# Hybrid decoder block: the turns of k and q taken two to a step, k's second high half written by ScalarE, two gate groups moved forward

## Chip, cores and metric

The kernel runs on one core of one Trainium2 chip. The metric is the device time of one execution in microseconds (us), the median of several runs; lower is better. A profile of one execution stands beside the times.

## The reference

One decoder layer on x of shape 1 x 1024 x 1024, all in float32:

```
h = RMSNorm(x);  [q | k | v | u | g] = h @ W_in
A: 8 heads, q and k split into two halves of 64, QK-norm per half,
   p = softmax(q1 k1' * scale + bias) - lam * softmax(q2 k2' * scale + bias), causal
   a = RMSNorm(p @ v) * (1 - lam_init);  y_a = a @ W_pa
B: c = silu(LayerNorm(conv31(u_a * sigmoid(u_b))));  y_b = c @ W_pc
x = x + (sigmoid(g_a) * y_a + sigmoid(g_b) * y_b) @ W_out
x = x + SwiGLU(RMSNorm(x))
```

## The kernel before

**Products in parts.** Every float32 operand is split into a high part (rounded to the type that TensorE multiplies, written by ScalarE, `split_hi`, L120) and a low part (the rest, by VectorE, `split_lo`, L125). A product is three matmuls, high x high, high x low, low x high (`mm3`, L160 to L162). Score products pack more: a tile of k holds 64 rows of high parts and 64 rows of low parts, so that two matmuls (L1017, L1018) make one score product of a half head.

**Stages.** From 0 to about 315 us the normalised x is turned and most of the input projection runs (`opening`, then the list `first`). From 315 to about 823 us the attention runs in 64 steps, 8 heads by 8 blocks of 128 queries, in the order 4 5 6 7 0 1 2 3 within a head (`ORDER`; the last head 6 7 4 5 2 3 0 1). Then come the projection of a, LayerNorm and the projection of c, W_out, and the feed-forward in seven-product form.

**A step** n of the attention (the loop after L1176) issues: the score products of its block (`scores`; VectorE adds the bias tile `tb` and takes the minimum at L1019, ScalarE the exponential at L1024, VectorE joins the halves at L1033); a *group* of filling work, a piece of the input projection that is still to be made (`more`); the transposes of the block before (`turn`, tile pT, then the split into ph and pl); and the `slot`: products with v (`weigh`, tile pW), transposes back (`back`, pB), the subln (`subln_T`, pS, whose result goes to a_d in HBM), and the *late* work.

**Groups.** The list `later` says which projections fill which head's steps. An item Q has 4 groups (48 matmuls of 256 columns each): the q and k columns of the next head, in two blocks b=1 and b=0 of 512 tokens. An item G has 2 groups: one column tile of the gates for each half of the tokens, 24 matmuls of 512 columns each. A head has 8 steps; `groups(n)` gives one group to a step, and none to two of the steps where the head's list has only 6. Groups left over after step 63 run in `group()` twice and then in a loop over the rest, between the end of the scores and the projection of a.

**Late work: the turn.** After the second and fourth group of an item Q, two entries join the list `late`: the turn of k and the turn of q of that block (`turn_qk`). The order is k b=1, q b=1, k b=0, q b=0. Each entry has a first step: k b=1 may go at once, q b=1 and k b=0 from the middle of the head before (step 4 of its 8), q b=0 from the first step of its own head. A slot takes one entry (`min(nq, 1)`). A turn is: 4 transposes of 128 columns into a PSUM tile pQ (L770); ScalarE writes the high part s1 (L777); VectorE writes the low part (L779); then copies by DMA, all issued on SyncE's queue, bring halves of 64 partitions to where the score products want them. For q there are six: s2's two halves and s1's lower half from s1 (L780, L786, L787), the same for the low parts (L785, L786, L787). For k there are three: the lower half of s2 from s1 (L780), the upper half of s2 from the low part (L790), and the lower half of s1 from the low part (L791). The last overwrites what the first reads, so it waits for it. A wait of SyncE holds up all that stands behind it in its queue.

The next head's bias tile `tb` (L996, one buffer) is loaded by SyncE after the last L1019 of the head. The rest of SyncE's queue near a head's start are the weights of later groups (`wraw`), v (L987), and what the groups write to HBM.

**After the scores.** `early(h)` (L1207) loads a of heads 0 to 5 back from a_d into tiles that had held scores, splits them (aTh, aTl), and heads 6 and 7 follow (L1240) when pS of head 7 has been written. The projection of a takes heads 0 to 7 in this order into four banks (`o3`).

**Order.** A scheduler orders each engine's instructions when the program is built, by its own estimates of time; each engine then runs its list strictly in that order. `issue_after` binds some of it.

Of the kernel before, what the change touches and what calls it, by code (L numbers as in the profile page):

```python
# [12 lines left out]
AF = mybir.ActivationFunctionType  # L13
# [7 lines left out]
HD = 64  # L21
# [10 lines left out]
NT = S // P  # L32
# [25 lines left out]
def kernel(  # L58
# [28 lines left out]
    dve, act, pool, pe = nc.vector, nc.scalar, nc.gpsimd, nc.tensor  # L87
# [24 lines left out]
    def nm(s):  # L112
        uid[0] += 1
        return f"{s}_{uid[0]}"

    def f32(ap):
        return ap.bitcast(F32)
# [9 lines left out]
    def after(ins):  # L127

        return nullcontext() if ins is None else tc.issue_after(ins)
# [16 lines left out]
    def pg():  # L146
        npg[0] += 1
        p_, tag = pgs[npg[0] % len(pgs)]
        return p_.tile([P, 512], F32, tag=tag, name=nm("pg"))
# [4 lines left out]
    def pm(z="pm"):  # L154
        npm[0] += 1
        p_, tag = pms[npm[0] % len(pms)]
        return p_.tile([P, 512], F32, tag=tag, name=nm(z))
# [82 lines left out]
    def pcol(key, k=0):  # L240
        c = col[key] + k
        return pvec[:, c : c + 1]
# [114 lines left out]
    def gemm_N(o, halves, shi, slo, i):  # L357

        ts = slice(i * P, (i + 1) * P)
        for k in range(NKT):  # L360
            whi, wlo = halves[k // 4]
            mm3(o, kt(shi, k)[:, ts], kt(slo, k)[:, ts], whi[:, k % 4, :], wlo[:, k % 4, :], k == 0, k == NKT - 1)
# [18 lines left out]
    first = ["U1", "V1", "U2", "U3", "V2", "U4", "Q0", "V3", "U5", "U6", "U7"]  # L381
    later = [
        ["Q1", "G0", "G1"],
        ["Q2", "G2"],
        ["Q3", "G3"],
        ["Q4", "G4", "G5"],
        ["Q5", "G6"],
        ["Q6", "G7"],
        ["Q7", "G8", "G9"],
        ["G10", "G11", "G12", "G13"],  # L390
        ["G14", "G15"],
    ]
    TAPS_FIRST = 3.25

# [245 lines left out]
    def rstd_of(ss, n, scale, fast=False):  # L640
        v = sm.tile([P, 16], F32, tag="v", name=nm("v"))[:, :n]
        dve.tensor_scalar(v, ss, scale, EPS, op0=ALU.mult, op1=ALU.add)
        return rsq(v, n, fast)
# [97 lines left out]
    def q_item(h):  # L741
        halves = [ws.next(), ws.next()]
        t = {}
        T[h] = t
        for b in (1, 0):
            raw = qkp.tile([P, 4, 256], F32, tag="qkraw", name=nm("qkraw"), bufs=2)
            ss = sm.tile([P, 16], F32, tag="ss16", name=nm("ss16"))
            for i2 in range(2):
                o = pg()
                for e in range(2):  # L750
                    gemm_N(o[:, 256 * e : 256 * (e + 1)], halves, hT_hi, hT_lo, 4 * b + 2 * i2 + e)
                act.copy(raw[:, 2 * i2 : 2 * i2 + 2, :], o[:].rearrange("p (e c) -> p e c", c=256))
                jk = sm.tile([P, VD], F32, tag="jk", name=nm("jk"), bufs=1)[:, :HD]
                for g in range(8):
                    act.activation(
                        jk, o[:, g * HD : (g + 1) * HD], AF.Square, accum_out=ss[:, 8 * i2 + g : 8 * i2 + g + 1]
                    )
                if i2 == 0:
                    yield
            r = rstd_of(ss[:], 16, 1.0 / HD, fast=h > 0)  # L760
            r4 = raw[:].rearrange("p i (g d) -> p (i g) d", d=HD)
            dve.tensor_tensor(r4, r4, r.unsqueeze(2).to_broadcast([P, 16, HD]), op=ALU.mult)

            def turn_qk(z, key, b, raw):


                dma = nc.sync.dma_start
                pt = pm("pQ")
                for i in range(4):
                    pe.transpose(pt[:, i * P : (i + 1) * P], raw[:, i, z * P : (z + 1) * P], ident[:])  # L770
                w = pcol(key + "n")

                def part(j):
                    return qkp.tile([P, 512], F32R, tag=f"{key}s{j}", name=f"{key}s{j}_{h}_{b}", bufs=2 if key == "q" else 3)

                s1, s2 = part(1), part(2)
                act.activation(s1[:], pt[:], AF.Identity, scale=w)  # L777
                lo = part(3) if key == "q" else qkp.tile([P, 512], F32R, tag="klo", name=f"klo_{h}_{b}", bufs=1)
                dve.scalar_tensor_tensor(lo[:], pt[:], w, f32(s1[:]), op0=ALU.mult, op1=ALU.subtract)  # L779
                dma(f32(s2[HD:, :]), f32(s1[HD:, :]))  # L780
                if key == "q":
                    lo2 = part(4)
                    for one, two in ((s1, s2), (lo, lo2)):
                        if one is lo:
                            dma(f32(two[HD:, :]), f32(one[HD:, :]))  # L785
                        dma(f32(two[:HD, :]), f32(one[HD:, :]))  # L786
                        dma(f32(one[HD:, :]), f32(one[:HD, :]))  # L787
                    t["q", b] = (s1, lo), (s2, lo2)
                else:
                    dma(f32(s2[:HD, :]), f32(lo[HD:, :]))  # L790
                    dma(f32(s1[HD:, :]), f32(lo[:HD, :]))  # L791
                    t["k", b] = s1, s2

            for z, key in ((1, "k"), (0, "q")):
                free = NT * (h - 1) + (0 if key == "k" and b else NT if key == "q" and not b else NT // 2)
                late.append((free if h else 0, lambda a_=(z, key, b, raw): turn_qk(*a_)))
            yield
# [156 lines left out]
    n = 0  # L956
# [130 lines left out]
    def subln(h):  # L1087
        an = AN[h]
        r = rstd_of(SSA[h][:], NT, 1.0 / VD, fast=True)
        dve.tensor_tensor(an[:], an[:], r.unsqueeze(2).to_broadcast([P, NT, VD]), op=ALU.mult)  # L1090
# [18 lines left out]
    steps = [(h, i) for h in range(H) for i in ORDER[h]]  # L1109
    scm, weighs, backs, sublns = [], [], [], []  # L1110
    fill = run(it for l_ in later for it in l_)
    plan = [sum(4 if it[0] == "Q" else 2 for it in l_) for l_ in later]
# [15 lines left out]
    def ready(queue, n):  # L1128
        now = [e for e in queue if e[0] <= n]
        queue[:] = [e for e in queue if e[0] > n]  # L1130
        return [e[1] for e in now]

    def slot(n, nq):

        with after(last_fill[0]):
            for h, b, ar in ready(backs, n):
                back(h, b, ar)
                if b == ORDER[h][-1] // 2:
                    subln(h)
                    sublns.append((n + 1, h))  # L1140
            for _ in range(min(nq, 1)):
                if late[0][0] <= n:
                    late.pop(0)[1]()
            for h in ready(sublns, n):
                subln_T(h)
            for h, b in ready(weighs, n):
                backs.append((n + 2, (h, b, weigh(h, b))))
                if b == ORDER[h][-1] // 2 and h + 1 < H:
                    load_v(h + 1)

    def groups(n):

        return 0 if plan[n // NT] == 6 and n % NT in (5, 7) else 1

    def slack_of(n):

# [11 lines left out]
    for n, (h, i) in enumerate(steps):  # L1168
# [3 lines left out]
        nq = len(late)  # L1172
# [14 lines left out]
    n = len(steps)  # L1187
# [162 lines left out]
    for c in range(NE, NKT):  # L1350
        w = ws.next()
# [400 lines left out]
```

## Time and profile before

| what | value |
|---|---|
| runs | 1771.92, 1770.11, 1770.12 us; median 1770.12 us |
| the profiled execution | 1771.98 us, its span of instructions 1770.1 us |
| TensorE matmul (PE) busy | 1751.4 us of the span, 99% |
| VectorE (DVE) busy | 1274.1 us, 72% |
| ScalarE (ACT) busy | 798.9 us, 45% |
| DMA | 274.81 MB, mean 155 GB/s |
| mean granted clock of TensorE | 0.996 |

How to read it: a matmul's busy time overlaps that of the next, so that its pace is the distance from start to start, not its duration. "PEld" is the weight load. An idle time is put down to what ended it. Times in the timeline are from the start of the span.

### The profile page before, as it was taken

To read this page: it belongs to the slowest core of one execution; us is meant where nothing else is said; L and a number is where in the kernel's file an instruction comes from. 1 tells how busy PE (TensorE), PEld (TensorE's weight loads), DVE (VectorE), ACT (ScalarE), POOL (GpSimd) and SP (SyncE) were. 2 spreads that over 40 slices of the span, in tenths; PEclk is the share of its full clock that TensorE was granted. 3 is DMA by queue.
4 is the path that set the end of the run, shared out by engine and by line. 5 is a ranking of instruction groups with operands and counts; after the bars stand their busy time and mean duration, and the time that the engine had idled before them with its cause. 6 is when DMAs were issued, how large, how long until landed. Compare 5 with 4: busy or idle time off the path is not lost.

```text
span 1770.1 us, 25847 instructions
## 1 busy us (share of the span) xinstructions
PE 1751.4 (99%) x9377; PEld 1508.0 (85%) x9377; DVE 1274.1 (72%) x2167; ACT 798.9 (45%) x1879; POOL 28.9 (2%) x107
## 2 busy tenths in 40 slices
PE   9999999999999999999999999999999999999999
PEld 7898998999898998988887888888888888888887
DVE  7388879999888988887587534877667666665544
ACT  5111331657766767655456413643333333333332
POOL 2001000000000000000000000000000000000000
PEclk9999999999999999999999999999999999999999
DMA  6236362244444344454783544234544544697663
GB/s 206 96 118 215 103 190 97 79 122 112 111 117 134 102 111 120 111 138 150 250 291 102 167 164 150 92 101 143 173 155 150 174 155 146 200 358 250 215 214 131
DMA packets 254867, 274.81 MB, mean 155 GB/s; under 512 B 15970, under 2 KB 177802, under 8 KB 254740
## 3 DMA queue, kind: packets, MB, share of 16 engines
q1 hardware_dynamic: 252560, 266.40, 47.5%
q0 software_dynamic: 1744, 5.19, 1.1%
q8 instruction: 74, 1.21, 0.3%
q10 hardware_dynamic: 436, 1.58, 0.2%
q14 instruction: 53, 0.43, 0.1%
HBM read 176.07 MB, written 78.68 MB: 144 GB/s over the span
## 4 chain that ended last, share of the span: by engine, by line
PE 92%; DMA 4%; DVE 2%; ACT 2%; issue 1%; SPq 0%; ACTq 0%
PE acc L1606 22%; PE pg L160 14%; PE pg L161 14%; PE pg L162 14%; PE acc L487 12%; PE sc L1017 2%; PE sc L1018 2%; PE wo L160 2%; PE wo L162 2%; PE wo L161 2%; PE pT L1056 2%; DMA ks<-ks 1%; DMA gt<-g_d 1%; PE pW L160 1%; PE pW L161 1%; PE pW L162 1%
## 5 line engine op out<-in xcount | busy, mean ns | idle before, releaser
L561 DVE SCALAR_TENSOR_TENSOR acc<-u,cw,acc 128x1024 f32<-128x1024 f32 x240 | 306.6, 1278 | 2.9
L120 ACT CAST whi<-wraw 128x1024 fp32r<-128x1024 f32 x107 | 112.4, 1052 | 204.7 <-PE pg L161 116.4
L160 PE MATMUL pg<-hT_hi,whi 128*128 128x512 f32 x512 | 201.9, 394 | 0.0
L162 PE MATMUL pg<-hT_hi,wlo 128*128 128x512 f32 x512 | 201.2, 393 | 0.0
L161 PE MATMUL pg<-hT_lo,whi 128*128 128x512 f32 x512 | 200.9, 392 | 0.0
L161 PE MATMUL pg<-wlo,hT_hi 128*128 128x256 f32 x704 | 200.7, 285 | 0.0
L160 PE MATMUL pg<-whi,hT_hi 128*128 128x256 f32 x704 | 200.7, 285 | 0.0
L162 PE MATMUL pg<-whi,hT_lo 128*128 128x256 f32 x704 | 200.4, 285 | 0.0
L125 DVE TENSOR_TENSOR wlo<-wraw,whi 128x1024 fp32r<-128x1024 f32 x107 | 130.2, 1218 | 68.5 <-ACT whi L120 68.4
L125 DVE TENSOR_TENSOR wlo<-draw,whi 128x1024 fp32r<-128x1024 f32 x75 | 91.8, 1224 | 89.4 <-ACT whi L120 87.1
L120 ACT CAST whi<-draw 128x1024 fp32r<-128x1024 f32 x75 | 79.1, 1055 | 129.6 <-PE acc L487 121.0
L161 PEld LDWEIGHTS pg<-wlo,hT_hi 128*128 128x128 f32 x704 | 134.9, 192 | 2.0
L160 PEld LDWEIGHTS pg<-whi,hT_hi 128*128 128x128 f32 x704 | 134.9, 192 | 1.8
L162 PEld LDWEIGHTS pg<-whi,hT_lo 128*128 128x128 f32 x704 | 134.8, 192 | 1.4
L487 PE MATMUL acc<-wlo,whi 128*128 128x512 f32 x308 | 119.8, 389 | 0.0
L487 PE MATMUL acc<-whi,wlo 128*128 128x512 f32 x308 | 119.8, 389 | 0.0
L1024 ACT ACTIVATE E<-E,mn 128x640 f32<-128x640 f32 (+7 forms) x128 | 99.4, 778 | 38.2 <-DVE mn L1019 37.4
L162 PEld LDWEIGHTS pg<-hT_hi,wlo 128*128 128x128 f32 x512 | 96.2, 188 | 19.1
L161 PEld LDWEIGHTS pg<-hT_lo,whi 128*128 128x128 f32 x512 | 96.3, 188 | 18.7 <-issue 0.6
L160 PEld LDWEIGHTS pg<-hT_hi,whi 128*128 128x128 f32 x512 | 96.3, 188 | 18.7 <-issue 0.6
L1606 PE MATMUL acc<-h_lo,whi 128*128 128x512 f32 x240 | 93.4, 389 | 0.0
L1606 PE MATMUL acc<-h_hi,whi 128*128 128x512 f32 x240 | 93.4, 389 | 0.0
(292 smaller groups left out, 4031.6 us busy)
## 6 DMA issues: line engine op xcount, KB each, us to landing
wraw<-in_w_gate_up_dram SPq DMA_DIRECT2D x44, 512.0 KB, 4.6
wraw<-in_w_in_dram SPq DMA_DIRECT2D x40, 512.0 KB, 4.1
qs<-qs SPq DMA_DIRECT2D x96, 128.0 KB, 2.3
wd<-in_w_down_dram SPq DMA_DIRECT2D x44, 256.0 KB, 3.2
tdT<-wd SPq DMA_DIRECT2D x88, 128.0 KB, 4.5
draw<-sdS SPq DMA_DIRECT2D x44, 256.0 KB, 3.8
draw<-tdT SPq DMA_DIRECT2D x44, 256.0 KB, 3.8
wraw<-in_w_in_dram SPq DMA_DIRECT2D x32, 256.0 KB, 3.6
```

What stands on the lines that cost most here:

```text
L120: act.copy(dst, src)
L125: last_lo[0] = dve.tensor_tensor(dst, src, f32(hi), op=ALU.subtract).ins
L160: pe.matmul(o, lh, rh, start=start, stop=False)
L161: pe.matmul(o, lh, rl, start=False, stop=False)
L162: last_mm[0] = pe.matmul(o, ll, rh, start=False, stop=stop).ins
L487: m = pe.matmul(o[s_][i][:], l_[:, ts], r_[:, 512:], start=start and j + y_ == 0, stop=j == n - 1 and y_ == 2, skip_group_check=not start,)
L561: dve.scalar_tensor_tensor(acc[0][:], us[c][:, t : t + S], cw[:, c, t : t + 1], acc[0][:], op0=ALU.mult, op1=ALU.add)
L1017: pe.matmul(o[:, :w], qh[:, qs], k, start=True, stop=False)
L1018: last_mm[0] = pe.matmul(o[:, :w], ql[:, qs], k, start=False, stop=True).ins
L1024: act.activation(e[:, :nk], e[:, :nk], AF.Exp, bias=mn[:, j : j + 1], scale=-1.0, accum_out=l[:, j : j + 1])
L1056: pe.transpose(pt[:, k * P : (k + 1) * P], e[:, (k0 + k) * P : (k0 + k + 1) * P], ident[:])
L1606: pe.matmul(o[:], a_[x_][:, k, :], b_[y_][:, k, :], start=start and k + x_ + y_ == 0, stop=k == 3 and x_ == 1, skip_group_check=not start,)
```

## The change

```diff
     later = [
         ["Q1", "G0", "G1"],
-        ["Q2", "G2"],
-        ["Q3", "G3"],
-        ["Q4", "G4", "G5"],
-        ["Q5", "G6"],
-        ["Q6", "G7"],
-        ["Q7", "G8", "G9"],
-        ["G10", "G11", "G12", "G13"],
-        ["G14", "G15"],
+        ["Q2", "G2", "G3"],
+        ["Q3", "G4"],
+        ["Q4", "G5", "G6"],
+        ["Q5", "G7"],
+        ["Q6", "G8", "G9"],
+        ["Q7", "G10"],
+        ["G11", "G12", "G13", "G14"],
+        ["G15"],
     ]
...
                 lo = part(3) if key == "q" else qkp.tile([P, 512], F32R, tag="klo", name=f"klo_{h}_{b}", bufs=1)
                 dve.scalar_tensor_tensor(lo[:], pt[:], w, f32(s1[:]), op0=ALU.mult, op1=ALU.subtract)
-                dma(f32(s2[HD:, :]), f32(s1[HD:, :]))
                 if key == "q":
+                    dma(f32(s2[HD:, :]), f32(s1[HD:, :]))
                     lo2 = part(4)
...
                 else:
+                    act.activation(s2[HD:, :], pt[HD:, :], AF.Identity, scale=w[HD:, :])
                     dma(f32(s2[:HD, :]), f32(lo[HD:, :]))
                     dma(f32(s1[HD:, :]), f32(lo[:HD, :]))
                     t["k", b] = s1, s2
...
-            for _ in range(min(nq, 1)):
+            for _ in range(min(nq, 2)):
                 if late[0][0] <= n:
                     late.pop(0)[1]()
...
-        return 0 if plan[n // NT] == 6 and n % NT in (5, 7) else 1
+        return 0 if plan[n // NT] == 6 and n % NT in (4, 6) or n == len(steps) - 1 else 1
```

A slot now takes up to two late entries, so that q b=1 and k b=0 of the next head go in the same step. The lower half of k's s2 is written by ScalarE from the PSUM tile, a second activation of 64 partitions by 512, and no longer by a DMA copy of s1: for each of the 16 turns of k one DMA less and one activation more. Two gate groups move from after the steps into the heads' lists; the last step has no group, so that 57 of the 60 groups run within the 64 steps (56 before) and 3 after them (4 before). The two steps without a group in a head of 6 groups are those of blocks 0 and 2 in place of 1 and 3. The sum of the products is the same.

## Prediction

> **What bounds the kernel now.** I read the page first, then the table of waits for TensorE, then the busy times stage by stage.
>
> ```profile
> span 1770.1 us, 25847 instructions
> PE 1751.4 (99%) x9377; PEld 1508.0 (85%) x9377; DVE 1274.1 (72%) x2167; ACT 798.9 (45%) x1879; POOL 28.9 (2%) x107
> ...
> PE sc L1017 <- DMA ks<-klo: 8.7, 4, 2.3
> ...
> 315.00:400.00 85.00, 85.00 (x597) 79.31 (x596) 80.55 (x163) 51.83 (x185) 1.40 (x8) 1.00 0.36 108
> 400.00:500.00 100.00, 97.50 (x674) 90.49 (x673) 89.17 (x221) 71.31 (x254) 2.16 (x12) 0.98 0.41 111
> 500.00:600.00 100.00, 97.84 (x682) 90.98 (x681) 84.76 (x201) 69.30 (x247) 2.71 (x15) 0.98 0.46 123
> 600.00:700.00 100.00, 97.69 (x693) 91.75 (x692) 87.30 (x209) 68.52 (x240) 2.18 (x12) 0.98 0.40 111
> 700.00:800.00 100.00, 97.96 (x577) 86.27 (x576) 85.06 (x192) 65.03 (x206) 2.17 (x12) 0.98 0.44 123
> 800.00:880.00 80.00, 80.00 (x407) 67.36 (x406) 51.78 (x96) 42.16 (x93) 1.29 (x7) 1.00 0.57 191
> ```
>
> TensorE bounds everything: busy 1751.4 of 1770.1 us. So a change pays only where TensorE stands or runs slowly. In the stages (length, then PE, PEld, DVE, ACT, POOL busy, granted clock, DMA share, GB/s) it never stands from 315 to 400 nor from 800 to 880, and once in each hundred between: 2.50 + 2.16 + 2.31 + 2.04 = 9.0 us. The table of waits names one cause: four times the first score product of a head waits for the last copy of k. The clock column says 0.98 in exactly these four, which is a second loss. A finer cut shows it:
>
> ```profile
> 450.70:452.80 2.10, 0.00 (x0) 0.00 (x0) 0.76 (x2) 2.00 (x12) 0.00 (x0) 1.00 0.28 66
> 454.10:457.50 3.40, 3.40 (x17) 3.38 (x16) 3.29 (x9) 2.22 (x9) 0.00 (x0) 0.50 0.13 29
> ...
> 706.80:710.10 3.30, 3.30 (x17) 3.30 (x16) 2.80 (x7) 2.79 (x13) 0.00 (x0) 0.50 0.29 67
> ```
>
> These are the first stop, the stretch after it, and the stretch after the last of the four; the two between look the same. After each stop TensorE runs 3.4 us at half its clock, so that half of it is lost: 1.7 us. The matmuls themselves show this from start to start: 0.21 us in the slow stretch, 0.12 us right after it.
>
> ```profile
> 444.29 0.60 PE L770 MATMUL pQ<-ident,qkraw 128*128 128x128 f32 x4
> ...
> 452.90 0.47 PE L1017 MATMUL sc<-ks,qs 128*128 128x512 f32 x1 [2.23 <-DMA ks<-klo]
> ...
> 456.47 0.41 PE L162 MATMUL pW<-ph,vl 128*128 128x256 f32 x1
> 456.68 0.41 PE L160 MATMUL pW<-ph,vh 128*128 128x256 f32 x1
> ...
> 457.77 0.28 PE L160 MATMUL pg<-whi,hT_hi 128*128 128x256 f32 x1
> 457.89 0.28 PE L161 MATMUL pg<-wlo,hT_hi 128*128 128x256 f32 x1
> ```
>
> The busy column counts the slow stretch as busy, so the four stops cost 9.0 + 4 x 1.7 = **15.8 us** in all. [...]
>
> The chain of waits tells how the first of the four comes about, with SyncE's own row:
>
> ```profile
> 444.93 0.69 ACT ks L777
> ...
> 446.21 4.33 DMA ks<-ks
> ...
> 450.56 2.21 DMA ks<-klo
> ```
> ```profile
> 445.43 0.69 SPq L996 DMA_DIRECT2D tb<-t_d  x1
> ```
>
> k's turn starts at 444.29 on TensorE and is usable at 452.9, 8.6 us later. Two copies stand one behind the other, 4.33 and 2.21 us; the first shares the DMA engines with the bias tile, issued 0.8 us before it.
>
> **The change part by part.**
>
> *k's high part by ScalarE.* The first copy leaves the chain, the largest term in it. What remains is measured in the same turn:
>
> ```profile
> 445.65 0.75 DVE L779 SCALAR_TENSOR_TENSOR klo<-pQ,pvec,ks 128x512 fp32r<-128x512 f32 x1 [0.20 <-ACT ks L777]
> ...
> 450.56 0.46 SPq L791 DMA_DIRECT2D ks<-klo  x1
> ...
> L777 ACT ACTIVATE ks<-pQ,pvec x16: 672/688/699, 227.4 to 761.3; 128x512 fp32r<-128x512 f32 x16
> ```
>
> From 444.29 to the end of klo are 2.1 us; two issues of 0.46 with gaps make 3.1; the copy's 2.2 us makes **5.3 us** in place of 8.6. The new activation reads 64 partitions and no row shows that form; it costs ScalarE between nothing and the 0.69 us of the full one, and I take 0.69, since both have 512 elements in a row: 16 x 0.69 = 11 us, on an engine busy 65 to 71% in these stages. It runs beside the two copies and is shorter than they. Without that cover it would hold pQ's bank 0.7 us longer. SyncE loses 16 issues of 0.46 us, worth nothing by themselves.
>
> *Two turns in one step.* In the built order I counted the matmuls between the turn of k b=0 and the next head's first score product, at the paces above (0.12 us for 256 columns; 0.23 for 512, below; 0.11, an estimate, for a transpose of 128). Before, for heads 1 to 7: 8.2, 5.2, 6.1, 7.3, 7.0, 5.8, 9.6 us. The four shortest, heads 2, 6, 3 and 5, are the four stops: the chain of 8.6 us doesn't fit in. After: 10.1, 7.5, 8.1, 9.9, 7.8, 7.1, 11.4. Against 5.3 us each head has 1.8 us or more to spare. But k's copies now stand on SyncE behind those of q, whose last ones wait for earlier ones to land:
>
> ```profile
> 438.52 0.60 PE L770 MATMUL pQ<-ident,qkraw 128*128 128x128 f32 x4
> ...
> 443.61 1.72 SPq L787 DMA_DIRECT2D qs<-qs  x2
> ```
>
> q's last issue ends at 445.33, 6.8 us after its turn. Two issues more (1.0 us) and 2.2 us to land make 10.0. From q's turn to the first score product the changed order has 10.8, 11.8, 11.2, 10.4, 11.0, 11.6, 12.7 us. So this fits in all seven, with 0.4 us at the tightest. I take 0.8 us in all for one or two heads that come late by under half a microsecond, which I count without a loss of clock; the bounds are nothing and rival C.
>
> *The bias tile* is late next:
>
> ```profile
> 440.26 0.40 PE L1018 MATMUL sc<-ks,qs 128*128 128x512 f32 x1
> ```
> ```profile
> 444.49 0.69 DVE L1019 CUSTOM_DVE_ANT_0 E<-sc,tb 128x512 f32<-128x512 f32 x1
> ```
> ```profile
> DMA to landing us min/median/max: 4.6/5.0/8.5
> ```
>
> Its copy (the last row gives the time to landing) is issued after the last L1019 of a head, which here ended 4.9 us after its product began. The fourth score tile of the new head needs the bank that the first L1019 frees. From the last product of the old head to that fourth tile stand, in the changed order, 14 to 19 us, and 8.6 once. Needed are 4.9 + 0.3 to the issue + 5.0 + 0.7 for one L1019 = 10.9, or 7.1 where VectorE follows its product at once. I cost it at nothing; rival B is this cover gone.
>
> *Groups moved.* Their matmuls cost the same anywhere, 24 x 0.23 = 5.5 us a group (853.38 to 853.61 below). One group fewer stands behind the scores, so that much cover goes from the chain that ends in the projection of a. That chain before:
>
> ```profile
> 835.54 0.38 PE L1056 MATMUL pT<-ident,E 128*128 128x128 f32 x2
> ...
> 853.38 0.39 PE L160 MATMUL pg<-aTh,whi 128*128 128x512 f32 x1
> 853.61 0.39 PE L161 MATMUL pg<-aTl,whi 128*128 128x512 f32 x1
> ...
> 858.60 1.03 PE L1097 MATMUL pS<-ident,an 128*128 128x128 f32 x8
> ```
> ```profile
> 831.41 4.86 SPq L1207 DMA_DIRECT2D early<-a_d  x4
> ```
> ```profile
> 842.23 1.05 ACT L120 CAST aTh<-early 128x1024 fp32r<-128x1024 f32 x1 [1.50 <-DMA early<-a_d]
> ...
> 865.51 1.94 ACT L120 CAST aTh<-at 128x512 fp32r<-128x512 f32 x3 [5.01 <-DMA at<-a_d]
> ```
> ```profile
> 836.72 0.43 DVE L125 TENSOR_TENSOR pl<-pT,ph 128x256 fp32r<-128x256 f32 x1 [1.33 <-ACT ph L120]
> ...
> 869.11 0.69 DVE L125 TENSOR_TENSOR aTl<-at,aTh 128x512 fp32r<-128x512 f32 x1 [0.94 <-ACT aTh L120]
> ```
>
> Three places lose it. (a) The last two transposes stand 0.9 us before the last product with v; from 835.54 the low part was done at 837.15, 1.6 us: 0.6 lost. (b) All four late copies of a now follow these transposes. Head 4's landed 6.7 us after them with one copy already under way; at about 2.2 us a copy (my estimate, 6.7 by three) head 5's lands after 10.9 and is cast 1.05 later, at 12.0. TensorE asks for it after 0.9 + 0.6 + 6 x 0.12 + 5.5 + 15 x 0.23 = 11.2: 0.8 us late, and as much again or more for the low part; I take 1.5. (c) From pS to the first product of head 6 the order leaves 0.9 + 27 x 0.23 = 7.1 us. The first cast started 6.9 us after pS and took 0.65, and VectorE's last low part ended 11.2 after: 0.4 us late at least and, by the low parts, 1.2 or so; I take 0.9. Together 3.0 us (bounds 0 and 7, if a stop of 2 us also takes the clock).
>
> *Sum.* -15.8 + 0.8 + 3.0 = **-12.0 us**. The profiled execution took 1771.98 us, 1.9 around its span; its span of 1770.1 would become 1758.1. The median of the runs is 1770.12, so I predict 1758.
>
> **The rivals.**
>
> A, *nothing is given back*: the tail's engines come earlier with the faster attention, and the spare times above hold. Then 1770.1 - 15.8 = 1754.3. For it: from 800 to 880 TensorE stood nowhere. Against: (a) to (c).
>
> B, *the bias tile takes the stop over*: VectorE is busy 85 to 89% in these stages, and 16 us fewer for the same work makes 90%; where it lags more than 5 us, the first L1019 waits for the tile and the fourth score tile for it. At four heads with 2 us each and no clock lost: 8 us back, 1766. The 8.6 us head speaks for it, the 14 to 19 us of the others against.
>
> C, *q's copies hold k's* (slower): if q's last issue ends later than 10.4 - 3.2 = 7.2 us after its turn, k is late at the tightest head. For the whole it decides when that issue ends some 10 us after the turn: then each of seven heads stops by 2 us or more and loses the clock, 7 x 4.0 = 28 us in place of 15.8: with the tail 1785. For it: eight copies in one queue, where a wait holds up all behind it. Against: the 6.8 us. [...]
>
> D, *the turn comes no earlier*: 1770. The counted order speaks against it.
>
> **How the numbers follow.** Forecast 0.55 (1754.5 to 1763 by its bounds), A 0.20, B 0.14, C 0.08, D 0.03. The range 1752 to 1768 takes in the forecast, A and B, and leaves out C, D and an edge of A. A measurement tells 0.2%, 3.5 us, from no change: faster than 1766.6 are the forecast, A and two thirds of B, 0.84; same the rest of B and D, 0.08; slower C, 0.08.
>
> **What will show it.** In the profile after: no wait of the score products for a copy of k in TensorE's table; PE busy 100 of 100 and clock 1.00 in the stages from 400 to 780; new waits for ph or pl, for aTh or aTl, of 0.5 to 2 us each between the last score product and the LayerNorm. It is wrong if the table again names ks or qs (C), if VectorE's L1019 waits for tb and TensorE with it (B), or if TensorE stands more than 7 us in the tail.

## The result, and the profile after

| | time, median | ratio to before | interval, 95% |
|---|---|---|---|
| before | 1770.21 us (6 runs) | | |
| after | 1765.62 us (1763.78 to 1766.47, 6 runs) | 0.9971 | 0.9958 to 0.9984 |

The change makes the kernel 4.6 us faster; 12 were forecast, and 1758 us. The sign is right and 1765.62 lies in the range, but almost two thirds of the expected gain are missing. The profiled execution took 1766.47 us. Its page begins:

```profile
span 1764.6 us, 25879 instructions
...
PE 1746.0 (99%) x9377; PEld 1503.3 (85%) x9377; DVE 1269.7 (72%) x2167; ACT 809.4 (46%) x1895; POOL 28.8 (2%) x107
```

The span is 5.5 us shorter. Where they come from is read by stages. Here are those of after (length, then PE, PEld, DVE, ACT, POOL busy, granted clock, DMA share, GB/s):

```profile
400.00:500.00 100.00, 100.00 (x673) 91.86 (x673) 89.38 (x217) 73.03 (x254) 2.16 (x12) 1.00 0.40 115
...
700.00:800.00 100.00, 100.00 (x626) 89.25 (x626) 86.69 (x199) 66.19 (x211) 2.16 (x12) 1.00 0.43 119
800.00:880.00 80.00, 71.73 (x354) 59.10 (x353) 57.00 (x106) 40.92 (x91) 1.28 (x7) 0.96 0.62 214
880.00:1000.00 120.00, 120.00 (x541) 99.16 (x540) 85.66 (x152) 66.05 (x104) 0.00 (x0) 1.00 0.53 175
...
1360.00:1560.00 200.00, 197.99 (x870) 162.92 (x869) 131.23 (x199) 67.08 (x91) 0.00 (x0) 1.00 0.56 182
```

From 400 to 800 us TensorE never stands and its clock is full (the two rows left out say the same): all four stops are gone. From 800 to 880, where it had not stood at all, it stands 8.3 us, and the clock is down to 0.96.

To count stops and slow clock together, I take each matmul's distance to the start of the next one, less the median of that distance for its shape, and sum this by stages. I call it *over the pace*. From 400 to 800 it falls from 18.1 to 1.0 us; from 800 to 880 it rises from 0.8 to 12.8; from 880 to 1000 it falls from 3.0 to 0.5; from 1360 to 1560 it rises from 0.8 to 2.8. Sum: -17.1 + 12.0 - 2.5 + 2.0 = -5.6, against the 5.5 by which the span is shorter.

TensorE's waits in the tail of after, 800 to 880 us (total, times, longest):

```profile
PE mean L1266 <- DVE lns L1264: 4.8, 1, 4.8
PE pT L1057 <- ACT jk L1086: 1.5, 1, 1.5
PE pB L1077 <- ACT ar L1071: 1.0, 1, 1.0
PE pW L160 <- ACT an L1085: 0.8, 1, 0.8
```

Before has no row in this table. The first is a product of the LayerNorm (the mean over channels) that waits for VectorE's sum. What follows it runs at half clock, as the start-to-start time of 0.43 us in the second and third row shows, against 0.23 in the fourth and fifth:

```profile
868.28 2.05 PE L1266 MATMUL mean<-lns,part 128*128 128x512 f32 x2 [4.84 <-DVE lns L1264]
...
870.98 0.63 PE L162 MATMUL pg<-aTh,wlo 128*128 128x512 f32 x1
871.41 0.63 PE L160 MATMUL pg<-aTh,whi 128*128 128x512 f32 x1
...
873.96 0.40 PE L160 MATMUL pg<-aTh,whi 128*128 128x512 f32 x1
874.19 0.40 PE L161 MATMUL pg<-aTl,whi 128*128 128x512 f32 x1
```
```profile
867.10:873.90 6.80, 5.62 (x11) 3.81 (x12) 6.80 (x12) 3.05 (x6) 0.00 (x0) 0.50 1.07 381
```

So 4.8 us of standing and 3.4 of slow clock are one stop, 8.2 of the 12.8 us. Three engines' own rows show what is late around it in after; the last matmul ahead of the stop starts at 863.05:

```profile
861.00 0.69 DVE L1264 TENSOR_TENSOR lns<-cT_lo 128x512 f32<-128x512 f32 x1 [0.87 <-DMA cT_lo<-c_d]
...
864.58 1.22 DVE L125 TENSOR_TENSOR wlo<-wraw,whi 128x1024 fp32r<-128x1024 f32 x1
...
866.32 1.22 DVE L125 TENSOR_TENSOR wlo<-wraw,whi 128x1024 fp32r<-128x1024 f32 x1
867.45 0.69 DVE L1264 TENSOR_TENSOR lns<-lns,cT_lo 128x512 f32<-128x512 f32 x1
868.05 2.48 DVE L1335 TENSOR_TENSOR gt<-pg,gt 128x512 f32<-128x512 f32 x4
```
```profile
862.80 2.00 ACT L120 CAST whi<-wraw 128x1024 fp32r<-128x1024 f32 x2 [3.40 <-PE pg L161]
864.81 1.28 ACT L1328 ACT_TABLE_LOAD   x1
866.11 2.19 ACT L1328 ACTIVATE gt<-gt 128x512 f32<-128x512 f32 x4
```
```profile
852.92 2.08 SPq L1241 DMA_DIRECT2D at<-a_d  x4
855.09 4.14 SPq L1262 DMA_DIRECT2D cT_lo<-c_d  x8
859.86 2.82 SPq L1327 DMA_DIRECT2D gt<-g_d  x4
```

VectorE adds up eight tiles of c, with two splits of weights between the additions, and only then does the gate multiplications (gt), which free the banks of the first four products of a. ScalarE makes the gates late too. And SyncE loads the gates behind eight loads of c, which stand behind the last loads of a. Which of these sets the stop, the profile alone does not tell; the first three theories below fell over it, wholly or in part.

### The profile page after: what moved, and what is told of

It reads as the page before. It is cut to its first block, busy times and chain, and to the rows that moved or that the text cites. A ratio compares the mean times of both kernels' runs of the same rounds, so it can differ in the third digit from the quotient of the medians.

```text
span 1764.6 us, 25879 instructions
## 1 busy us (share of the span) xinstructions
PE 1746.0 (99%) x9377; PEld 1503.3 (85%) x9377; DVE 1269.7 (72%) x2167; ACT 809.4 (46%) x1895; POOL 28.8 (2%) x107
## 4 chain that ended last, share of the span: by engine, by line
PE 94%; DMA 3%; DVE 2%; ACT 1%; issue 0%; SPq 0%; DVEq 0%; ACTq 0%
PE acc L1607 20%; PE pg L160 15%; PE pg L161 15%; PE pg L162 15%; PE acc L487 12%; PE sc L1019 2%; PE sc L1018 2%; PE pT L1057 2%; PE wo L161 2%; PE wo L160 2%; PE wo L162 2%; PE pW L160 1%; PE pW L161 1%; PE pW L162 1%; PE pg L844 1%; PE pQ L770 1%
```

## The experiments

All eighteen, with the time over the pace by stages (us), and the groups of gate products left in TensorE's order when the last but one step's scores begin. Each ratio is to runs of before on the same chip; before's median was 1768.0 to 1770.5 us there, so that rows are better compared by ratio than by time. The stage figures are of one profiled execution each, which need not be like the median: f2's took 1765.69 us against 1768.76, e13's 1756.21 against 1758.01.

| kernel | groups left | time, us | ratio (95%) | 400-800 | 800-880 | 880-1000 | 1360-1560 |
|---|---|---|---|---|---|---|---|
| before | 6.0 | 1770.21 | | 18.1 | 0.8 | 3.0 | 0.8 |
| after | 3.0 | 1765.62 | 0.9971 (0.9958 to 0.9984) | 1.0 | 12.8 | 0.5 | 2.8 |
| e1_turn_only | 6.0 | 1757.43 | 0.9929 (0.9917 to 0.9942) | 4.3 | 0.7 | 1.0 | 0.5 |
| e2_groups_only | 3.2 | 1768.83 | 0.9992 (0.9983 to 1.0002) | 5.2 | 12.6 | 0.5 | 0.6 |
| e3_copy_only | 6.0 | 1758.29 | 0.9934 (0.9920 to 0.9947) | 5.0 | 0.7 | 2.2 | 0.5 |
| e4_two_only | 6.0 | 1758.40 | 0.9934 (0.9921 to 0.9948) | 4.1 | 1.5 | 2.2 | 1.0 |
| e6_three_less_behind | 2.8 | 1766.66 | 0.9990 (0.9981 to 0.9999) | 1.0 | 13.0 | 1.0 | 1.7 |
| e7_four_behind | 4.0 | 1763.54 | 0.9973 (0.9962 to 0.9983) | 1.0 | 10.6 | 0.5 | 2.1 |
| e8_mean_later | 3.0 | 1765.27 | 0.9983 (0.9974 to 0.9991) | 1.1 | 13.6 | 0.5 | 1.5 |
| e9_groups_four_behind | 4.0 | 1768.53 | 0.9998 (0.9988 to 1.0007) | 6.2 | 11.6 | 0.5 | 0.6 |
| e10_five_left | 5.0 | 1766.08 | 0.9991 (0.9982 to 1.0001) | 4.4 | 8.8 | 0.5 | 4.4 |
| e11_last_step_free | 6.0 | 1758.56 | 0.9942 (0.9923 to 0.9961) | 4.1 | 4.7 | 1.0 | 0.5 |
| e12_seven_left | 6.7 | 1761.21 | 0.9960 (0.9944 to 0.9976) | 4.9 | 4.6 | 0.5 | 1.9 |
| e13_skips_4_6 | 5.5 | 1758.01 | 0.9938 (0.9924 to 0.9952) | 5.0 | 0.9 | 0.5 | 0.5 |
| e14_sum_later | 3.0 | 1764.36 | 0.9978 (0.9968 to 0.9988) | 1.0 | 10.8 | 1.3 | 1.4 |
| f1_order_mended | 3.0 | 1769.58 | 1.0014 (1.0004 to 1.0024) | 1.0 | 10.8 | 6.2 | 1.7 |
| f2_five_order_mended | 5.0 | 1768.76 | 1.0001 (0.9991 to 1.0011) | 4.4 | 6.5 | 4.8 | 0.6 |
| g1_gates_loaded_first | 3.0 | 1761.29 | 0.9952 (0.9939 to 0.9965) | 1.0 | 4.9 | 4.1 | 1.7 |
| g4_five_gates_first | 5.0 | 1762.00 | 0.9953 (0.9939 to 0.9966) | 4.4 | 2.0 | 4.1 | 2.2 |
| g3_skips_4_6_gates_first | 5.5 | 1759.57 | 0.9941 (0.9928 to 0.9954) | 7.1 | 1.5 | 1.8 | 0.6 |

### The parts of the change, one by one

e1 is after with the list `later` and the line of `groups` as in before. e2 is before with only these two changed:

```diff
-        ["Q2", "G2"],
+        ["Q2", "G2", "G3"],
...
-        return 0 if plan[n // NT] == 6 and n % NT in (5, 7) else 1
+        return 0 if plan[n // NT] == 6 and n % NT in (4, 6) or n == len(steps) - 1 else 1
```

e3 is before with the copy replaced, e4 is before with `min(nq, 2)`:

```diff
-                dma(f32(s2[HD:, :]), f32(s1[HD:, :]))
                 if key == "q":
+                    dma(f32(s2[HD:, :]), f32(s1[HD:, :]))
...
+                    act.activation(s2[HD:, :], pt[HD:, :], AF.Identity, scale=w[HD:, :])
```

> The kernel after with the old list of gate groups: the second high half by ScalarE and two late entries a slot stay, the groups are not moved, so four groups stand behind the last scores as before. Theory (the turn removes the four stops of heads 2, 3, 5 and 6, and the moved groups make the stop of about 5 us in the tail, because the LayerNorm's first mean product then comes too soon in TensorE's order): 400 to 800 us without a stop of sc for k's copy, 17 us less of start-to-start time than before; the mean product waits under 1 us and 800 to 880 is within 3 us of before; 1753 to 1757 us. Rival (the stop in the tail comes of the faster attention itself, with VectorE and ScalarE behind at its end): the mean product waits 3 us or more again, 1762 to 1767 us. Second rival (the stops need the moved groups as well): at least one stop of sc for k's copy stays, 1760 to 1766 us.

> The kernel before with the new list of gate groups alone: the copy by DMA and one late entry a slot stay. Theory: the stops of sc for k's copy stay at the heads where the distance from the turn to the scores is short (15 us or so of loss), and the LayerNorm's mean product waits 3 us or more in the tail, with one more half-clock stretch: 1775 to 1783 us, slower than before. Rival (the moved groups alone push the scores away from the turns and so remove stops): 400 to 800 us has 8 us or more less idle time than before, 1760 to 1770 us. Rival (the stop in the tail comes of the faster attention, not of the groups): the mean product waits under 1 us here, 1768 to 1772 us.

> The kernel before with k's second high half by ScalarE alone; one late entry a slot and the old list stay. Theory (the DMAs behind the turn lie one after the other on SyncE's queue, and one fewer of them shortens the way from k's turn to the scores by about 3 us, more than the 1.4 to 2.7 us by which the four stops are late): at most one stop stays, 1754 to 1759 us, most of the gain by this part alone. Rival (the way is not shortened, since k's low half is what lands last and its place is set by VectorE): three or four stops stay, 1765 to 1771 us.

> The kernel before with two late entries a slot alone; the copy by DMA and the old list stay. Theory (the second turn of a head comes a slot of 1.8 us or so sooner, against stops of 1.4 to 2.7 us, but q's DMAs then stand on SyncE's queue in front of or between k's): one to three of the four stops stay, 1757 to 1766 us. Rival (the two parts are only good together): all four stay or grow, 1768 to 1785 us. Rival (the sooner turn is all of the gain): none stays, 1753 to 1757 us.

Without the moved groups the kernel takes 1757.43 us, faster than after. The stage of e1 in which after stands:

```profile
800.00:880.00 80.00, 80.00 (x385) 66.70 (x384) 51.85 (x85) 41.36 (x86) 0.93 (x5) 1.00 0.70 246
```

So the stop of the tail comes of the moved groups, not of the faster attention: the first rival falls. The attention is where the theory was too bold: it gave 17 us of pace, e1 gains 13.8, and its time is 0.4 us above the range. It keeps 4.3 us over the pace in small waits, where after keeps 1.0: the moved groups are worth up to 3.3 us there.

The copy alone and the second late entry alone each remove the four stops: 400 to 800 us has 5.0 and 4.1 us over the pace in place of 18.1, and of the waits for k one of 0.5 us is left in e3 and none in e4, more than I gave e4. They are two remedies for one ill, and together bring no more than either (1757.43 against 1758.29 and 1758.40; the intervals overlap). The waits of e3 from 400 to 800 show one price of the new activation: once TensorE waits for it, since it holds the bank of pQ.

```profile
PE pW L160 <- ACT ks L790: 1.4, 1, 1.4
PE sc L1018 <- DMA ks<-klo: 0.5, 1, 0.5
```

The moved groups alone (e2) are a third remedy: the scores come later behind the turn, and less is waited for k. But the tail takes the same amount back, and the time is that of before (0.9992). So what I expected of e2's stops was wrong, and its rival right. Its waits from 400 to 900 us:

```profile
PE mean L1265 <- DVE lns L1263: 4.6, 1, 4.6
PE sc L1017 <- DMA ks<-klo: 2.6, 4, 1.4
PE pg L160 <- ACT aTh L120: 2.1, 1, 2.1
```

### First theory of the tail: the mean product comes too soon

Between the last pS (the end of the subln) and the mean product stand 51 products of a in after, 73 in before (single matmuls of 512 columns). e6, e7 and e8 are after with

```diff
e6
+        return 0 if plan[n // NT] == 6 and n % NT in (4, 6) else 1
e7
+        return 0 if plan[n // NT] == 6 and n % NT in (4, 6) or n >= len(steps) - 2 else 1
e8
+        with after(None if sb else last_mm[0]):
+            pe.matmul(mean[:], part[:], s1[:], start=True, stop=True)
...
+        os2 = [gemm_T(w, aT_hi, aT_lo, 0)]
+        if c == NE:
+            ln_step()
         ln_step()
```

and e9 is e2 with the condition of e7.

> The kernel after with one more group among the steps and one less behind them: two groups (48 products) stand behind the last scores where after has three and before has four; 32 products of a stand between the last pS and the first mean product, where after has 51 and before has 73. Theory (the stop in the tail is a race: the LayerNorm sum is ready some 9.7 us plus 5.0 to 7.1 us after the last pS, TensorE comes to the mean product after so many products at 0.23 us each): TensorE comes there 7.4 us behind pS, so the waits between pS and the mean product rise from 5 us to 8 to 9.5 us in sum, with one more half-clock stretch; 1769 to 1775 us. Rival (the stop has a fixed cause that has nothing to do with the number of products in front, such as the loads of c): the wait stays at 5 us, 1764 to 1768 us.

> The kernel after, with all parts of the change, but with four groups behind the scores as in before (the last two steps take none); the groups are still moved forward among the earlier steps. 78 products stand between the last pS and the first mean product. Theory (cover of 78 x 0.226 = 17.6 us against 15 to 16 us needed): the mean product waits under 1 us, 800 to 880 within 2 us of before, no stop of sc; 1753 to 1758 us. Rival (moving the groups itself costs in the tail, wherever the last one stands): 1761 us or more.

> The kernel after with its groups as they are, but the first mean product is held behind one further half of a product with a (24 products), so that 75 stand between the last pS and it, where after has 51; the LayerNorm sum and the weight splits between its additions stay as they are in VectorE's order. Theory (only TensorE's place for the mean product is wrong, not the sum's own time): the sum is still ready 16.8 us or so behind the last pS, TensorE comes after 75 x 0.228 = 17.1 us; the wait falls from 4.8 to under 1 us, the half-clock stretch goes, and the later LayerNorm is covered by the other products; 1756 to 1760 us. Rival (the LayerNorm is then late at a later point, where its output is needed): the wait goes but comes back behind 870 us, 1762 to 1767 us.

> The kernel before (the copy by DMA, one late entry a slot) with the new list of groups, but four groups behind the scores. Theory (the moved groups alone put the scores of heads 2, 3, 5 and 6 further from the turns, as the earlier run of the groups alone showed with 2.6 us of waits in place of 8.7; what that run lost again was only the tail): 400 to 800 us as in that run, 4 to 5 us over the pace in place of 18, and no wait of the mean product; 1757 to 1761 us. Rival (the groups that go back to the tail leave the scores as near to the turns as before): the four stops come back, 1766 to 1771 us.

None gave the time of the theory; all four times lie in the ranges of the rivals, e9's not for its rival's reason, since its attention keeps 6.2 us over the pace and not 18. In e8, where only the mean product is held back, TensorE stands at the same place for something else (waits from 800 to 1000 us):

```profile
PE pg L160 <- DVE gt L1338: 6.3, 1, 6.3
PE pT L1057 <- ACT jk L1086: 1.5, 1, 1.5
PE pW L160 <- ACT an L1085: 0.8, 1, 0.8
```

The next product of a needs a bank that a gate multiplication frees, and this stands behind the sum. So the mean product was only the first in TensorE's order to meet the delay. In e7 the mean product comes without a wait, as the theory says, but the last two steps now have no group, and TensorE stands there (waits from 800 to 815 us):

```profile
PE sc L1018 <- DVE mn L1020: 1.8, 1, 1.8
PE pW L160 <- DVE pl L125: 1.4, 1, 1.4
PE pS L1098 <- ACT at L1100: 0.8, 1, 0.8
```

e9 does the same with one wait of 5.1 us for VectorE's E and two of 1.3 and 1.1 us. In e6 waits for aTh (two, 3.4 us), for a gate multiplication (1.7) and for the sum (1.6) share the loss. The sum of the loss hardly changes, 10.6 to 13.6 us, while its place does.

### Second theory: filling work is lacking, and it is paid somewhere

e10 to e13 are e1 with one step more or fewer in the line of `groups`:

```diff
e10
+        return 0 if plan[n // NT] == 6 and n % NT in (5, 7) and n != 5 * NT + 7 else 1
e11
+        return 0 if plan[n // NT] == 6 and n % NT in (5, 7) or n == len(steps) - 1 else 1
e12
+        return 0 if plan[n // NT] == 6 and n % NT in (5, 7) or n == 6 * NT + 7 else 1
e13
+        return 0 if plan[n // NT] == 6 and n % NT in (4, 6) else 1
```

> The turn parts with the old list (the first experiment), but one of the eight steps without a group gets one: head 5's last. So 5 groups (120 products of the gates) are left in TensorE's order when the scores of the last but one step begin; the first experiment and before have 6, after has 3, the versions with four groups behind the scores and none in the last two steps have 4. Theory (from there to the LayerNorm the chain through softmax, transposes, subln and reload of a has a length of its own, and what TensorE lacks of filling work against it is stood off somewhere, now at one place, now at another; 6 groups are just enough): about one group of 5.5 us is lacking, 800 to 880 is 4 to 8 us over the pace, 1761 to 1765 us. Rival (only the fixed places of the moved groups of after cost, the number left does not matter): 800 to 880 under 2 us over, 1756 to 1759 us.

> The turn parts with the old list, and the last step takes no group, as in after: 5 groups behind the scores in place of 4, and still 6 left when the scores of the last but one step begin. Theory (the number left decides): as the first experiment, 800 to 880 within 1.5 us of the pace, 1756 to 1759 us. Rival (the step without a group is the cause, since its scores stand there uncovered): 800 to 880 loses 3 us or more, 1760 us or more.

> The turn parts with the old list, and head 6's last step takes no group: between 6 and 7 groups left when the scores of the last but one step begin. Theory (6 are enough, more only lengthens a cover that nobody waits for): 800 to 880 within 1 us of the pace, 1755 to 1759 us, as the first experiment. Rival (each group left is worth its share, the stop being only hidden in other places): 3 us or more faster than the first experiment, 1752 to 1754 us.

> The turn parts with the old list of groups, but the steps without a group are those of blocks 0 and 2, as in after: 5.5 groups left when the scores of the last but one step begin. Theory (number left decides): half a group is lacking, 800 to 880 is 1 to 4 us over the pace; the attention keeps its pace as in after; 1756 to 1760 us. Rival (the changed steps without a group are what costs): 1762 us or more.

The number counts, but not alone. With 5 left the stop is back, and larger than a group's 5.5 us (e10: the mean product waits 5.7 us, 8.8 over the pace). With 5.5 there is none. But e11 and e12, with 6 and 6.7 left, lose 4.7 and 4.6 us, by a wait of 2.1 and 2.0 us for a gate multiplication that stands behind other work on VectorE. Their times are as the theory had it for e11 and 2 us above for e12; e10's is 1 us above. A count of groups does not explain that.

### Third theory: the order on VectorE and ScalarE

e14 is after with the sum behind the four gate multiplications and the mean product behind 48 more matmuls. f1 has besides, bound by hand, the four gate sigmoids in front of ScalarE's two weight casts and the gate multiplications in front of the two weight splits; f2 does this to e10.

```diff
e14
+            with after(None if sb else last_gt[0]):
+                dve.tensor_tensor(s1[:], cc[0] if c == 1 else s1[:], cc[c], op=ALU.add)
f1
+            with after(last_sum[0] if sb else last_gt[0]):
+                add = dve.tensor_tensor(s1[:], cc[0] if c == 1 else s1[:], cc[c], op=ALU.add).ins
...
+        with after(last_gt[0] if c == NE else None), after(last_sig[0] if c == NE else None):
+            w = ws.next()
```

Here `last_gt` is the last gate multiplication, `last_sig` the last gate sigmoid, `last_sum` the last addition of the other half's sum.

> The kernel after with VectorE's LayerNorm sum held behind the four gate multiplications that free the banks of the projection of a, and the mean product held behind two further products (48 matmuls); the two weight splits still stand in front of the gate multiplications, and on ScalarE the two casts for them still stand in front of the gates' sigmoids. Theory (the stop is made by the order of VectorE and ScalarE at the end of the first four products of a: the next one needs a bank that a gate multiplication frees, and this stands behind work that itself waits for those products' end): the sum no longer holds TensorE, but the banks do: a wait of 3 to 5 us for a gate multiplication stays, 1762 to 1766 us. Rival (what is lacking is filling work, and the stop goes wherever it must): a stop of 4.5 to 6.5 us in all. Second rival (the sum alone was the cause): no stop, 1756 to 1758 us.

> The kernel after, groups and turn as they are (3 groups left when the scores of the last but one step begin), with the order at the end of the first four products of a bound by hand: ScalarE's four gate sigmoids in front of the two weight casts, VectorE's four gate multiplications in front of the LayerNorm sum and of the two weight splits, the mean product behind two further products of a. Theory (order: nothing that TensorE then needs soon stands behind work that waits for TensorE): no stop from 855 to 880; what stays in 800 to 880 are the three waits of 1.5, 1.0 and 0.8 us from the last steps, 3 to 4.5 us over the pace in place of 12.8; 1755 to 1759 us. Rival (lack of filling work: the chain from the last scores has a length of its own, and moving groups away must be paid): 8 us or more over the pace still stand somewhere between 800 and 1000, 1763 us or more.

> The version with 5 groups left (the turn parts, the old list, one step more with a group), with the same order bound by hand as in the last run. Theory (order): 800 to 880 under 2 us over the pace in place of 8.75, 1756 to 1759 us. Rival (lack of filling work): 5 us or more over the pace between 800 and 1000, 1762 us or more.

It fell as well. e14 waits 4.1 us for the gate multiplication, as was said of it; but with the whole order mended the wait is still there (4.6 us in f1, 4.3 in f2), and the LayerNorm, now later, costs 6.2 and 4.8 us from 880 to 1000. Both times, 1769.58 and 1768.76, lie in the rival's ranges. f1's rows show why:

```profile
865.81 2.61 ACT L1337 ACTIVATE gt<-gt 128x512 f32<-128x512 f32 x4 [4.65 <-DMA gt<-g_d]
```
```profile
852.36 2.09 SPq L1241 DMA_DIRECT2D at<-a_d  x4
854.54 5.01 SPq L1262 DMA_DIRECT2D cT_lo<-c_d  x8
860.57 2.28 SPq L1336 DMA_DIRECT2D gt<-g_d  x4
```

ScalarE had nothing in front of the sigmoids any more, and waited 4.65 us for the gates themselves. SyncE issued them at 860.57, behind the eight loads of c, and they took 5.2 us to land.

### Fourth theory: SyncE's queue

g1 is after with one move: the gates of the first two columns are loaded between the loads of a and those of c. g4 does it to e10, g3 to e13.

```diff
+    with after(last_at):
+        g3 = [[gated(g_d[c], slice(sb * 512, (sb + 1) * 512)) for sb in range(2)] for c in range(2)]
+    last_at = last_of(mybir.EngineType.SP)
```

> The kernel after with one move: SyncE loads the gates of the first two columns right behind the loads of a of heads 6 and 7 and in front of the eight loads of c, where after has them behind these. By it the gate sigmoids come in front of the two weight casts on ScalarE and the gate multiplications in front of the LayerNorm sum on VectorE, and the mean product moves behind 110 products. Groups as in after (3 left). Theory (queue: the banks that the next product of a needs are freed by gate multiplications, whose gates stand on SyncE's queue behind the loads of c, which wait for the last pS; in after, in the run with the order mended and in the run with the sum later the gates were issued 9.3 to 10 us behind pS and landed 5.2 us later, past the end of the first four products of a): gates issued 4 us behind pS, no stop of 3 us or more from 855 to 880, 800 to 880 is 3 to 5 us over the pace, the later LayerNorm gives back 0 to 4 us before 1000; 1755 to 1761 us. Rival (lack of filling work that must be paid anywhere): 8 us or more over the pace between 800 and 1000, 1762 us or more.

> The version with 5 groups left (8.75 us over the pace from 800 to 880, mean product waiting 5.7 us), with the same single move of the gates' loads. Theory (queue): no stop of 3 us or more from 855 to 880, 800 to 880 under 2 us over the pace, up to 4 us given back before 1000; 1756 to 1761 us. Rival (lack of filling work): 5 us or more over the pace from 800 to 880, 1763 us or more.

> The version with the turn parts, the old list and no group in the steps of blocks 0 and 2 (1758.0 us, no stop in the tail), with the same single move of the gates' loads. Theory (queue): nothing was waiting for the gates there, so nothing is won and the later LayerNorm may cost 0 to 4 us; 1757 to 1762 us. Rival (the loads of c and the gates crowd each other, and the move frees the queue in general): 2 us or more faster, 1754 to 1756 us.

The stop is gone, in both kernels that had it. Rows of g1 on TensorE (the last pS), SyncE and VectorE, and its waits of TensorE from 800 to 1000 us:

```profile
850.79 1.03 PE L1098 MATMUL pS<-ident,an 128*128 128x128 f32 x8
```
```profile
853.14 2.11 SPq L1241 DMA_DIRECT2D at<-a_d  x4
855.30 2.60 SPq L1251 DMA_DIRECT2D gt<-g_d  x4
858.00 6.49 SPq L1274 DMA_DIRECT2D cT_lo<-c_d  x9
```
```profile
862.18 2.49 DVE L1341 TENSOR_TENSOR gt<-pg,gt 128x512 f32<-128x512 f32 x4 [2.12 <-PE pg L162]
```
```profile
PE pg L160 <- ACT cT_hi L120: 1.6, 2, 1.1
PE pT L1057 <- ACT jk L1086: 1.5, 1, 1.5
PE pB L1077 <- ACT ar L1071: 1.1, 1, 1.1
PE pW L160 <- ACT an L1085: 0.8, 1, 0.8
```

VectorE no longer waits for the gates but for the products themselves. What stays are the three waits of the last steps, which after has too, and one for cT_hi, which before had as well (1.5 us): c now loads and is normalised later, and 4.1 us over the pace come back before 1000 us. Net, g1 takes 1761.29 us, 0.3 above what was expected, and 800 to 880 falls from 12.8 to 4.9 us with the groups where after has them. In g4 it falls from 8.8 to 2.0, again with 4.1 before 1000; its time is 1.0 above what was expected. In g3, which had no such stop, the move wins nothing (0.9941 against e13's 0.9938).

So the stop goes when the gates stand ahead of c in SyncE's queue. The move takes the order of ScalarE and VectorE with it, and the mean product goes behind 110 products. But f1 has that order without the queue, and keeps the stop; the queue's place alone, with after's order, was not run. The rival, filling work that must be paid anyhow, is out for this stop only. Its sign for g1, 8 us or more over the pace between 800 and 1000, is met: 4.9 + 4.1 = 9.0 us stay of after's 13.3; only its time, 1762 us or more, is missed by 0.7. And in the last steps e7 and e9 stood in the scores that had no group.

Why before did not stop can now be read from its rows:

```profile
869.08 2.26 SPq L1326 DMA_DIRECT2D gt<-g_d  x4
```
```profile
874.97 1.36 DVE L1334 TENSOR_TENSOR gt<-pg,gt 128x512 f32<-128x512 f32 x2
```
```profile
876.07 1.02 PE L1265 MATMUL mean<-lns,part 128*128 128x512 f32 x2
876.52 0.80 PE L160 MATMUL pg<-aTh,whi 128*128 128x512 f32 x1
```

There too the gates stand behind c in the queue. The first gate multiplication ends at 875.66, 17.1 us behind the start of the last pS (858.60), and the next product of a starts at 876.52, behind the mean products: 0.9 us to spare, with 73 products of a between pS and there. In after the last pS is here:

```profile
850.57 1.03 PE L1098 MATMUL pS<-ident,an 128*128 128x128 f32 x8
```

Its first gate multiplication ends at 868.74, 18.2 us later, a chain of nearly the same length. But only 51 products cover it, because others had to fill the place of the groups before pS. The 22 that are missing are worth 22 x 0.23 = 5.1 us; with 1.1 more of chain and 0.9 to spare before, TensorE should come 5.3 us too soon, and the stop is 4.8. In g1 the cover is the same 51 products, and the chain is 12.1 us.

This count sorts the kernels where the groups left did not. With 72 to 79 products between pS and the next product that needs a bank (before, e1, e3, e4, e7, e9, e13) none has such a stop. With 32 to 52 (after, e2, e6, e8, e10, e14, f1, f2) all have one, unless the gates are loaded first (g1 and g4, 51 and 52 products, chains of 12.1 and 12.8 us, where the others of these two lists have 16.7 to 19.1). In e11 and e12 all 96 products of the first four banks stand behind pS; their gate multiplications are late for another reason, the LayerNorm's subtractions in front of them on VectorE. And in g3 the gates land early, but additions of the LayerNorm stand in front of the multiplications: its chain is 18.0 us, and 73 products cover it. So the gates' place in the queue is worth some 6 us of the chain, and is not the whole of it.

e1, the change without its groups, has the lowest ratio: 1757.43 us, 0.9929 (0.9917 to 0.9942). e3, e4 and e13 cannot be told from it.

## Why the prediction was wrong, step by step

- **The four stops, -15.8.** Right. All are gone, and the lost clock with them: 17.1 us of pace. The distances held within 0.2 us for k and q in all seven heads: k's are 7.1 to 11.5 us in after. The way of k held less well: where the trace tells the last landing (heads 1, 2, 3 and 6) it is 8.8, 5.7, 6.3 and 5.1 us behind the turn, against 5.3; the spare time covered that. What I did not see is that the steps overlap: the copy, the second entry and the moved groups each shorten the same four waits (e3, e4, e2). So the groups added at most 3.3 us to the gain of the other two, and their price in the tail was 12.0.
- **k and q late, +0.8.** Nothing of it showed (1.0 us over the pace in all from 400 to 800).
- **The bias tile, 0.** Right: no product waits for it, and VectorE waits for it once, 1.3 us.
- **The new activation at the full 0.69 us.** Right: 0.68 us for 64 partitions.

```profile
L790 ACT ACTIVATE ks<-pQ,pvec x16: 682/683/687, 230.8 to 761.2; 64x512 fp32r<-64x512 f32 x16
```

- **"Groups moved", +3.0.** This is the step that failed: it measured +12.0. Two things in it were wrong. It counted "one group fewer" behind the scores. But the last step loses its group too, and in TensorE's order 72 gate products are left when the last but one step's scores begin, where before has 144: three groups. And it followed the chain only to the first product of head 6, by places (a) to (c). (a) showed with 0.8 us at the last product with v, where 0.6 was forecast; waits of 1.5 us at 814.84 and 1.0 at 832.44, both at transposes of the last steps, were not in it. (b) and (c) did not show, no wait for aTh or aTl is there. The place that cost 8.2 us is one link further, at the end of the first four banks of the projection of a, which are freed by gate multiplications whose gates SyncE loads behind c: 18.2 us from pS, with products for some 13 us to cover it. The prediction's list of what hangs behind pS stops before it. By its own sign, "TensorE stands more than 7 us in the tail", it is wrong: the four waits make 8.1.
- **What lay outside the sum.** The LayerNorm's end came without the wait of before (880 to 1000: -2.5, and given back wherever the LayerNorm was moved later: f1, f2, g1, g4). The feed-forward lost 2.0: at 1533 us VectorE waits 8.99 us for a load of the down weights, and one product of TensorE for VectorE 2.0. Nine of the eighteen kernels have 1.4 to 4.4 us over the pace there, the other nine at most 1.0. What decides it no run tells; it stays open.

## What to carry to other kernels

Before summing the gains of several edits, ask whether they cure the same wait: then one is enough, and the others only bring their prices. Filling work moved forward is taken from a chain behind it; follow that chain through every queue to the point where banks or buffers come free, SyncE's queue too, and compare its length with the products that are left to cover it (here 18.2 us against 51 products of 0.23 us). And when holding back the instruction that waits only moves the wait to another one, look for what both hang on.

## What the runs showed of the hardware

In these runs the clock that went with a short stop was not fixed by the stop's length. The four stops of before (8.7 us in all, the longest 2.3) took half the clock for 3.4 us each. In e11 one of 2.1 us, the only one from 800 to 880, shows a clock of 0.98 over these 80 us; my estimate from these two numbers is 2 x 0.02 x 80 = 3.2 us at half:

```profile
800.00:880.00 80.00, 77.90 (x365) 64.43 (x364) 52.16 (x84) 41.07 (x84) 0.93 (x5) 0.98 0.72 252
```

In e12 one of 2.0 us, again the only one there, shows 0.98 too. But the one of 2.0 us in the feed-forward of after shows 1.00 over 200 us, and 1.00 from its end at 1534.39 to 1538.90. Behind the 1.5 us that end at 814.84 the clock reads 1.00 up to 822.00 as well. With the stop of 4.8 us in after went 6.8 us at half the clock, and these account for the stage's 0.96.

Nor was it the same from one execution of a kernel to the next. Of the 102 executions of before that stand beside the experiments, ten have a mean granted clock of 0.996 and took 1770.4 to 1773.7 us; five have 1.000 and took 1763.8 to 1765.6. Four stretches of 3.4 us at half clock are 6.8 us lost in 1770, a mean of 0.996; by that reckoning those five lost hardly any, though no trace of one is kept. The 15.8 us of the prediction is thus the price of the stops in an execution like the profiled one; without the clock, by the same sum, it is 9.0.
